# SSD mixer of a two-layer trunk: scores and decay as one product on a zero-padded tile, small copies on ScalarE, the transposed state in two tiles, no copy of the stacked rows

## The chip, the core and the metric

The kernel runs on one core of a Trainium2 chip. The metric is the device time of one execution in microseconds, the median of several runs. Engines are called TensorE (PE in the rows; PEld is its weight load), VectorE (DVE), ScalarE (ACT), GpSimd (POOL) and SyncE (SP, which issues most DMAs).

## What is computed

The reference is one inference step of a two-layer trunk on 512 prompt tokens and 8 x 8 sample tokens, 576 columns in all. Each layer has a SwiGLU block, a mixer, and another SwiGLU block. The mixer of layer 0 is the Mamba-2 SSD mixer that the change touches:

```python
def ssd_mixer(h, ssm0, conv0, w_in, conv_w, conv_b, dt_bias, a_log, d_skip, norm_g, w_out):
    proj = h @ w_in
    z, xbc, dt_raw = jnp.split(proj, [D_INNER, D_INNER + CONV_DIM], axis=-1)
    xbc, conv_new = causal_dwconv(xbc, conv0, conv_w, conv_b)      # width 4
    xbc = jax.nn.silu(xbc)
    xs, Bm, Cm = jnp.split(xbc, [D_INNER, D_INNER + SSD_GROUPS * D_STATE], axis=-1)
    ...
    y, ssm_new = ssd_scan(xs, dt, A, Bm, Cm, ssm0)
    y = y + d_skip.astype(f32)[:, None] * xs.astype(f32)
    y = y.reshape(bsz, l, D_INNER) * jax.nn.silu(z.astype(f32))
    yg = y.reshape(bsz, l, SSD_GROUPS, D_INNER // SSD_GROUPS)
    yg = yg * lax.rsqrt(jnp.mean(yg * yg, axis=-1, keepdims=True) + EPS)
    ...
# in ssd_scan, by chunks of 128 prompt tokens (8 for the samples):
    decay = jnp.exp(jnp.where(tril, seg, -jnp.inf))
    cb = jnp.einsum('bclgn,bcsgn->bclsg', Cc, Bc)
    y_diag = jnp.einsum('bclsgr,bcsgrp->bclgrp', cb[..., None] * decay, xdt)
    chunk_states = jnp.einsum('bcsgn,bcsgr,bcsgrp->bcgrpn', Bc, decay_end, xdt)
    h_final, h_starts = lax.scan(step, h_init, ...)
    y_off = jnp.einsum('bclgn,bclgr,bcgrpn->bclgrp', Cc, jnp.exp(a_cum), h_starts)
```

There are 8 groups of 4 heads; a head has 64 channels and a state of 64 x 128. New states, the last three rows before the convolution, and the token outputs are returned.

## The kernel before

Activations lie with channels on the 128 partitions and the 576 tokens along a row. The weights are read in float32 and split on the chip into a high and a low part (`block`: a cast on ScalarE, L317, and a subtraction, L318, which in this mixer GpSimd mostly does). A projection of one block of 128 channels (`proj`, `mm`, `passes`) is 48 matmuls of 288 columns into one of two PSUM accumulators (`acc`, two banks each); the split weights go through six buffers, two to a projection.

`ssd` loops over the groups g = 0 to 7. `conv_in(ct)` projects one block of the 32 convolved channel blocks. VectorE moves it out of the accumulator into `ext` (L637 to L639), in which the halo, the three rows before each sample sequence, is set in front (L636). The last three rows of each sequence go into `tails` (L641, L642). Then comes the convolution in `cacc`: one step on ScalarE (L645) and three on VectorE (L647). `ext` has two buffers.

`group(bt, ctl)` makes, once for each group, B transposed (`bnat`), the stacked B rows of the samples split into two parts (`bns`, `bsp`) and spread by a mask (`bblk`, GpSimd), and the scores `cbs` of B and C: 512 columns for the prompt and 64 x 64 for the samples.

`pair(g, j)` treats two heads at a time, 16 in all. It loads the state `nat`, transposes it on TensorE (L789) and copies it into `h0t`, one half by ScalarE and one by VectorE (L790); eight small matmuls of C with it (L795) follow. The decays `m` come by DMA, are masked on GpSimd (L808 to L810), put through the exponential on ScalarE (L813) and multiplied by the scores on VectorE (L814, L815); the products with `xdt` are L871 and L873. The running state of the chunks is `ht` (L853, L857), used by L864.

Groups 2, 4 and 6 also run eight blocks of the output projection (`outproj`, with `yn`), four ahead of each pair, each a unit of 24 matmuls (12 in group 2) that VectorE adds to `x` (L414), which frees the accumulator. The sum of squares of a group is `sqacc` (L949), which TensorE reduces over the partitions (L184). `spread` (L749) uses `rhs`, the end of a long chain on the step sizes in group 0.

No order is written out for most of this. A scheduler with a timeline of its own sets the order of each engine's instructions when the program is built, so any edit in the mixer can move others. Each engine then works through its own list in order.

Of the kernel before, what the change touches and what calls it, by code (L numbers as in the profile page):

```python
# [8 lines left out]
F32 = mybir.dt.float32  # L9
F32R = mybir.dt.float32r  # L10
I32 = mybir.dt.int32
AF = mybir.ActivationFunctionType
ALU = mybir.AluOpType
# [4 lines left out]
P = 128  # L18
D = 1024
KD = D // P  # L20
SEQ = 512
NB = 8
# [27 lines left out]
def trunk(ctx, tc, x_prompt, x_sample, state_ssm, state_conv, state_pool,  # L50
# [536 lines left out]
    def ssd(tail):  # L587
# [5 lines left out]
        with ExitStack() as st:  # L593
# [37 lines left out]
            def conv_in(ct):  # L631
# [4 lines left out]
                V.tensor_copy(out=es[:, :, 0:3], in_=cst[:, ct].rearrange("p (b e) -> p b e", e=3))  # L636
# [5 lines left out]
                V.tensor_copy(out=tails[:, ct, 3:27].rearrange("p (b e) -> p b e", e=3), in_=es[:, :, XST - 3:XST])  # L642
# [136 lines left out]
            def pair(g, j, bt, ctl, bnat, bblk, cbs, xst, yt):  # L779
# [5 lines left out]
                h0t = wk.tile([P, NB, P], F32, name="h0t", bufs=1)  # L785
                for q in range(2):
                    pt = misc()
                    for i in range(4):
                        PE.transpose(out=pt[:, i * P:(i + 1) * P], in_=nat[:, 4 * q + i], identity=ident)  # L789
                    (V.tensor_copy if q else S.copy)(out=h0t[:, 4 * q:4 * q + 4], in_=pt.rearrange("p (b n) -> p b n", n=P))  # L790
                pq = misc()
                for b in range(NB):
                    r = b % 4 * 32
                    o = SEQ + b // 4 * 32
                    PE.matmul(out=pq[r:r + 32, (2 + b // 4) * P:(3 + b // 4) * P], lhsT=ctl[:, o:o + 32], rhs=h0t[:, b], start=True, stop=True)  # L795
# [18 lines left out]
                V.tensor_tensor(out=m[:, :, 0:SEQ], in0=m[:, :, 0:SEQ], in1=cbs[:, 0:SEQ].unsqueeze(1).broadcast_to([P, 2, SEQ]), op=ALU.mult)  # L814
                V.tensor_tensor(out=ms, in0=ms, in1=cbs[0:64, SEQ:T].unsqueeze(1).broadcast_to([64, 2, 64]), op=ALU.mult)  # L815
# [101 lines left out]
            def group(bt, ctl):  # L917
                bnat = gp.tile([P, 4, P], F32, name="bnat")
                bns = gp.tile([96, 2, P], F32, name="bns")
                bsp = gp.tile([96, 2, P], F32, name="bsp")  # L920
                bblk = gp.tile([96, 2, 4, P], F32R, name="bblk")
                cbs = gp.tile([P, T], F32, name="cbs")
# [6 lines left out]
                S.copy(out=bns, in_=pt[0:96, 0:2 * P].rearrange("s (q n) -> s q n", q=2))  # L929
                S.copy(out=bsp.bitcast(F32R), in_=bns)  # L930
                V.tensor_tensor(out=bsp[32:64].bitcast(F32R), in0=bns[32:64], in1=bsp[32:64], op=ALU.subtract)
# [8 lines left out]
                S.copy(out=cbs[0:64, SEQ:T], in_=pt[0:64, 0:64])  # L940
                return bnat, bblk, cbs
# [30 lines left out]

            ys = None
# [246 lines left out]
```

## Time and profile before

| | us |
|---|---|
| median of 3 runs | 2354.91 (2354.45 to 2358.41) |
| profiled execution, its own time | 2357.4 |
| its span, first to last instruction | 2355.6 |
| TensorE busy | 2282.7 (97%) |
| VectorE busy | 1874.8 (80%) |
| ScalarE busy | 1053.1 (45%) |
| GpSimd busy | 1030.7 (44%) |

The mixer's work lies between about 428 and 1003 us. A row of the profile groups instructions by source line, engine and operands; after the bar it gives their busy time, the mean of one, and how long the engine stood idle just before them and for whom. A wait names the instruction that came last.

### The profile page before, as it was taken

What the parts mean: (1) busy time and instruction counts of PE and PEld (TensorE: products, weight loads), DVE (VectorE), ACT (ScalarE), POOL (GpSimd) and SP (SyncE); (2) the same over time, 40 slices, a digit from 0 to 9 for tenths busy, and PEclk for the clock granted to TensorE, in tenths of its full rate; (3) what the DMA queues carried; (4) which work ended last, traced back from release to release, by engine and by line L of the source; (5) the groups of instructions that cost most, each with busy time, mean ns of one, the idle gap of its engine ahead of it and who ended that gap; (6) DMA issues with size and microseconds to landing.
All of it is one profiled execution on the core that took longest, in us unless ns stands there. A gap on an engine that the chain in (4) does not pass through costs nothing.

```text
span 2355.6 us, 43789 instructions
## 1 busy us (share of the span) xinstructions
PE 2282.7 (97%) x17572; PEld 2241.3 (95%) x17572; DVE 1874.8 (80%) x2950; ACT 1053.1 (45%) x1947; POOL 1030.7 (44%) x796
## 2 busy tenths in 40 slices
PE   8999999999999999989999999999999999999998
PEld 7999999988999999979999999999999899999997
DVE  8987778688887786798877799778876859778876
ACT  6444434455554545354444354334444344344433
POOL 4555440344444444155554535555531325555530
PEclk9999999999999999999999999999999999999999
DMA  5223222243443334412232232323222242322221
GB/s 150 90 90 108 81 90 66 62 138 110 134 135 107 118 110 113 116 57 88 90 108 82 89 99 72 108 64 99 90 81 67 67 117 83 108 68 94 90 73 59
DMA packets 272904, 222.23 MB, mean 94 GB/s; under 512 B 8322, under 2 KB 269042, under 8 KB 272701
## 3 DMA queue, kind: packets, MB, share of 16 engines
q1 hardware_dynamic: 269172, 218.04, 30.4%
q8 instruction: 139, 2.28, 0.4%
q10 hardware_dynamic: 3528, 1.39, 0.2%
q14 instruction: 65, 0.52, 0.1%
HBM read 206.46 MB, written 12.94 MB: 93 GB/s over the span
## 4 chain that ended last, share of the span: by engine, by line
PE 60%; DVE 9%; ACT 1%; DMA 1%; issue 1%; DVEq 0%; SPq 0%; ACTq 0%
PE acc L375 29%; PE acc L339 27%; DVE wh L256 1%; PE acc L554 1%; DVE cacc L647 1%; PE acc L479 1%; DVE ws L1102 1%; DVE m L814 0%; DMA rd<-in_pool_w_out 0%; PE misc L871 0%; DVE wb L318 0%; PE misc L851 0%; PE misc L864 0%; DVE glo L256 0%; ACT m L813 0%
## 5 line engine op out<-in xcount | busy, mean ns | idle before, releaser
L375 PE MATMUL acc<-wh,wb 128*128 128x288 f32 x6888 | 920.4, 295 | 4.2 <-DVE fo L380 2.3
L375 PEld LDWEIGHTS acc<-wh,wb 128*128 128x128 f32 x6888 | 916.1, 189 | 5.9 <-ACT wb L317 3.2
L339 PE MATMUL acc<-ghi,wb 128*128 128x288 f32 x2752 | 550.7, 295 | 0.3 <-DVE x L416 0.3
L339 PEld LDWEIGHTS acc<-ghi,wb 128*128 128x128 f32 x2752 | 441.2, 188 | 0.6 <-DVE x L416 0.5
L317 ACT CAST wb<-raw 128x512 fp32r<-128x512 f32 (+1 forms) x440 | 265.7, 607 | 358.8 <-PE acc L339 151.9
L339 PE MATMUL acc<-glo,wb 128*128 128x288 f32 x1376 | 404.2, 295 | 0.0
L339 PE MATMUL acc<-hhi,wb 128*128 128x288 f32 x1824 | 382.8, 300 | 2.3 <-DVE x L414 0.8
L318 POOL TENSOR_TENSOR wb<-raw,wb 128x512 fp32r<-128x512 f32 (+1 forms) x154 | 211.3, 1374 | 339.5 <-ACT wb L317 330.5
L318 DVE TENSOR_TENSOR wb<-ws,wb 128x512 fp32r<-128x512 f32 x328 | 325.8, 1004 | 15.0 <-ACT wb L317 14.9
L318 DVE TENSOR_TENSOR wb<-raw,wb 128x512 fp32r<-128x512 f32 (+1 forms) x286 | 269.3, 956 | 63.8 <-ACT wb L317 63.3
L317 ACT CAST wb<-ws 128x512 fp32r<-128x512 f32 x328 | 202.5, 621 | 241.0 <-PE acc L375 216.8
L339 PEld LDWEIGHTS acc<-hhi,wb 128*128 128x128 f32 x1824 | 297.8, 190 | 5.7 <-issue 1.6
L416 DVE SCALAR_TENSOR_TENSOR x<-acc,x 128x576 f32<-128x576 f32 x160 | 120.6, 754 | 194.8 <-PE acc L339 194.6
L339 PE MATMUL acc<-hlo,wb 128*128 128x288 f32 x912 | 273.4, 300 | 0.0
L356 POOL TENSOR_TENSOR ws<-raw,ws 128x512 f32<-128x512 f32 x82 | 151.9, 1852 | 246.0 <-DVE wb L318 241.0
L339 PEld LDWEIGHTS acc<-glo,wb 128*128 128x128 f32 x1376 | 257.9, 188 | 0.0
L318 POOL TENSOR_TENSOR wb<-rd,wb 128x512 fp32r<-128x512 f32 x128 | 174.8, 1374 | 184.0 <-ACT wb L317 183.8
L317 ACT CAST wb<-rd 128x512 fp32r<-128x512 f32 x196 | 114.0, 592 | 250.1 <-PE acc L339 219.3
L355 POOL TENSOR_TENSOR ws<-raw 128x512 f32<-128x512 f32 x82 | 124.6, 1520 | 160.4 <-DVE wb L318 160.4
L339 PEld LDWEIGHTS acc<-hlo,wb 128*128 128x128 f32 x912 | 173.0, 190 | 0.8 <-issue 0.2
L353 POOL TENSOR_TENSOR ws<-raw 128x512 f32<-128x512 f32 x82 | 128.4, 1566 | 87.5 <-DMA raw<-in_ffn_w_gate 78.4
L354 POOL TENSOR_TENSOR ws<-ws,raw 128x512 f32<-128x512 f32 x82 | 130.3, 1589 | 7.7 <-DVE wb L318 1.5
(329 smaller groups left out, 2897.5 us busy)
## 6 DMA issues: line engine op xcount, KB each, us to landing
raw<-in_ffn_w_gate SPq DMA_DIRECT2D x41, 1024.0 KB
raw<-in_ffn_w_up SPq DMA_DIRECT2D x41, 1024.0 KB
rd<-in_ffn_w_down SPq DMA_DIRECT2D x80, 512.0 KB
raw<-in_ssd_w_in SPq DMA_DIRECT2D x48, 512.0 KB
m<-ad SPq DMA_DIRECT2D x16, 576.0 KB
nat<-in_state_ssm SPq DMA_DIRECT2D x16, 512.0 KB
out<-nat SPq DMA_DIRECT2D x16, 512.0 KB
raw<-in_ssd_w_out SPq DMA_DIRECT2D x24, 256.0 KB
```

Of the source, the lines that this page charges most:

```text
L256: V.scalar_tensor_tensor(out=o, in0=xs, scalar=g, in1=sub, op0=ALU.mult, op1=ALU.subtract)
L317: S.copy(out=hi, in_=src)
L318: (eng or V).tensor_tensor(out=lo, in0=src, in1=hi.bitcast(F32), op=ALU.subtract)
L339: PE.matmul(out=pd[:, h, 0:HALF], lhsT=lt, rhs=a[:, h * HALF:(h + 1) * HALF], start=first and n == 0, stop=last and n == 3 * len(acts) - 1)
L353: G.tensor_tensor(out=s[0], in0=blk[2], in1=blk[3], op=ALU.add)
L354: G.tensor_tensor(out=s[1], in0=s[0], in1=blk[0], op=ALU.subtract)
L355: G.tensor_tensor(out=s[2], in0=blk[2], in1=blk[0], op=ALU.subtract)
L356: G.tensor_tensor(out=s[3], in0=blk[1], in1=s[1], op=ALU.subtract)
L375: PE.matmul(out=pt[:, m, 0:HALF], lhsT=wb[:, j, k], rhs=hh[k, h][:, slot], start=n == 0, stop=n == 11)
L416: V.scalar_tensor_tensor(out=halves(x[:, d]), in0=pt[:, :, 0:HALF], scalar=scale, in1=halves(x[:, d]), op0=ALU.mult, op1=ALU.add)
L479: PE.matmul(out=pd[:, m, 0:HALF], lhsT=w[:, a, 2 * k + m], rhs=b[:, h * HALF:(h + 1) * HALF], start=n == 0, stop=n == 5)
L554: PE.matmul(out=pt[:, m, 0:HALF], lhsT=wb[:, a, k], rhs=hh[k, b][:, slot], start=q == 0 and k == a == b == 0, stop=q == 1 and k == 3 and a ...
```

## The change

Five edits, all in `ssd`:

- The halo copy into `ext` (L636) and the copy of the samples' last rows into `tails` (L642) go from VectorE to ScalarE, 32 of each.
- `h0t` becomes two tiles of four sequences each instead of one tile of eight.
- `cbs` is one tile for all groups, whose lower right corner (partitions 64 to 127 of the samples' columns) is set to zero once, so that the decays are multiplied by the scores in one operation of 128 x 2 x 576 instead of two. The samples' scores are copied into it by VectorE instead of ScalarE.
- `bns` is gone. ScalarE casts the stacked rows from PSUM, and VectorE's subtraction reads them from there as well.

```diff
                 G.memset(ext[:, 0:3], 0.0)
-                V.tensor_copy(out=es[:, :, 0:3], in_=cst[:, ct].rearrange("p (b e) -> p b e", e=3))
+                S.copy(out=es[:, :, 0:3], in_=cst[:, ct].rearrange("p (b e) -> p b e", e=3))
...
                 S.copy(out=tails[:, ct, 0:3], in_=ext[:, SEQ:SEQ + 3])
-                V.tensor_copy(out=tails[:, ct, 3:27].rearrange("p (b e) -> p b e", e=3), in_=es[:, :, XST - 3:XST])
+                S.copy(out=tails[:, ct, 3:27].rearrange("p (b e) -> p b e", e=3), in_=es[:, :, XST - 3:XST])
...
-                h0t = wk.tile([P, NB, P], F32, name="h0t", bufs=1)
+                h0t = [wk.tile([P, 4, P], F32, name=f"h0t{k}", bufs=1) for k in range(2)]
...
-                    (V.tensor_copy if q else S.copy)(out=h0t[:, 4 * q:4 * q + 4], in_=pt.rearrange("p (b n) -> p b n", n=P))
+                    (V.tensor_copy if q else S.copy)(out=h0t[q], in_=pt.rearrange("p (b n) -> p b n", n=P))
...
-                V.tensor_tensor(out=m[:, :, 0:SEQ], in0=m[:, :, 0:SEQ], in1=cbs[:, 0:SEQ].unsqueeze(1).broadcast_to([P, 2, SEQ]), op=ALU.mult)
-                V.tensor_tensor(out=ms, in0=ms, in1=cbs[0:64, SEQ:T].unsqueeze(1).broadcast_to([64, 2, 64]), op=ALU.mult)
+                V.tensor_tensor(out=m, in0=m, in1=cbs.unsqueeze(1).broadcast_to([P, 2, T]), op=ALU.mult)
...
-                S.copy(out=bns, in_=pt[0:96, 0:2 * P].rearrange("s (q n) -> s q n", q=2))
-                S.copy(out=bsp.bitcast(F32R), in_=bns)
-                V.tensor_tensor(out=bsp[32:64].bitcast(F32R), in0=bns[32:64], in1=bsp[32:64], op=ALU.subtract)
+                S.copy(out=bsp.bitcast(F32R), in_=pt[0:96, 0:2 * P].rearrange("s (q n) -> s q n", q=2))
+                V.tensor_tensor(out=bsp[32:64].bitcast(F32R), in0=pt[32:64, 0:2 * P].rearrange("s (q n) -> s q n", q=2), in1=bsp[32:64], op=ALU.subtract)
...
-                S.copy(out=cbs[0:64, SEQ:T], in_=pt[0:64, 0:64])
-                return bnat, bblk, cbs
+                V.tensor_copy(out=cbs[0:64, SEQ:T], in_=pt[0:64, 0:64])
+                return bnat, bblk
...
+            cbs = gp.tile([P, T], F32, name="cbs")
+            V.memset(cbs[64:P, SEQ:T], 0.0)
             ys = None
             for g in range(8):
```

The new source is two lines shorter, so from L815 on an instruction has a slightly smaller line number in the new program (L931 becomes L927, L949 becomes L945). The rebuilt order differs in many places in the mixer. Three of them follow.

VectorE at the start of group 1, before; `sqacc` is the sum of squares, `m` the decays, `rm` and `rr` the inverse root of the norm:

```order
L949 TENSOR_TENSOR sqacc<-sqacc,sq 128x576
L937 COPY cbs<-misc 128x512
L931 TENSOR_TENSOR bsp<-bns,bsp 32x256
L814 TENSOR_TENSOR m<-m,cbs 128x2x512 x2
L815 TENSOR_TENSOR m<-m,cbs 64x2x64 x2
L189 TENSOR_SCALAR rm<-misc 128x5
L190 TENSOR_SCALAR rr<-rm 128x5
L192 TENSOR_TENSOR rt<-rr 128x5
L790 COPY h0t<-misc 128x512
```

and now:

```order
L945 TENSOR_TENSOR sqacc<-sqacc,sq 128x576
L927 TENSOR_TENSOR bsp<-misc,bsp 32x256
L933 COPY cbs<-misc 128x512
L936 COPY cbs<-misc 64x64
L814 TENSOR_TENSOR m<-m,cbs 128x1152 x2
L189 TENSOR_SCALAR rm<-misc 128x5
L190 TENSOR_SCALAR rr<-rm 128x5
L790 COPY h0t_5916<-misc 128x512
```

Both pairs' multiplies stand together; the samples' scores now come from VectorE itself, just ahead of them, and the two L815 are gone.

VectorE at the start of group 4, before; `ext` is read out of the accumulator of a projection, `acc_8319` is that of the first block of the output projection:

```order
L937 COPY cbs<-misc 128x512
L647 SCALAR_TENSOR_TENSOR cacc<-ext,cw,cacc 128x600
L814 TENSOR_TENSOR m<-m,cbs 128x2x512 x2
L931 TENSOR_TENSOR bsp<-bns,bsp 32x256
L647 SCALAR_TENSOR_TENSOR cacc<-ext,cw,cacc 128x600
L637 TENSOR_TENSOR ext<-acc_8231,rb 128x288
L949 TENSOR_TENSOR sqacc<-sqacc,sq 128x576
L638 TENSOR_TENSOR ext<-acc_8231,rb 128x224
L639 TENSOR_TENSOR ext<-acc_8231,rb 128x8x8
L815 TENSOR_TENSOR m<-m,cbs 64x2x64 x2
L636 COPY ext<-cst 128x8x3
L414 TENSOR_TENSOR x<-acc_8319,x 128x576
```

and now, where the same block is `acc_8306`:

```order
L923 COPY bnat<-misc 128x512
L647 SCALAR_TENSOR_TENSOR cacc<-ext,cw,cacc 128x600
L927 TENSOR_TENSOR bsp<-misc,bsp 32x256
L933 COPY cbs<-misc 128x512
L945 TENSOR_TENSOR sqacc<-sqacc,sq 128x576
L637 TENSOR_TENSOR ext<-acc_8218,rb 128x288
L638 TENSOR_TENSOR ext<-acc_8218,rb 128x224
L639 TENSOR_TENSOR ext<-acc_8218,rb 128x8x8
L936 COPY cbs<-misc 64x64
L814 TENSOR_TENSOR m<-m,cbs 128x1152 x2
L414 TENSOR_TENSOR x<-acc_8306,x 128x576
```

The sum and the reads of the accumulator have moved ahead of the two multiplies.

ScalarE a little later in group 4, before; `xst` is the activated x block, `s` a stack of its sample columns:

```order
L913 ACT_TABLE_LOAD
L913 ACTIVATE xst<-cacc 128x512
L914 ACTIVATE xst<-cacc 128x64
L317 CAST wb<-raw 128x512
L775 COPY s_8504<-xst 128x192
L641 COPY tails<-ext 128x3
L645 ACTIVATE cacc<-ext,cols,cw 128x600
```

and now:

```order
L912 ACT_TABLE_LOAD
L912 ACTIVATE xst<-cacc 128x512
L913 ACTIVATE xst<-cacc 128x64
L636 COPY ext<-cst 128x8x3
L317 CAST wb<-raw 128x512
L641 COPY tails<-ext 128x3
L642 COPY tails<-ext 128x24
L645 ACTIVATE cacc<-ext,cols,cw 128x600
```

The halo copy stands behind an activation and ahead of a weight cast, the tail copy ahead of the first step of the convolution.

## Rows read from the trace of the kernel before

**Rows 1.** Stretch table: length, busy PE, PEld, DVE, ACT, POOL; clock; DMA.

```profile
428.00:1003.00 575.00, 551.35 (x4552) 524.40 (x4552) 456.58 (x1013) 287.39 (x615) 233.70 (x222) 0.98 0.40 116
```

**Rows 2.** Waits of TensorE from 428 to 1003: total us, times, longest.

```profile
PE misc L795 <- DVE h0t L790: 5.1, 3, 2.5
PE misc L749 <- DVE rhs L744: 4.9, 1, 4.9
PE acc L339 <- DVE ext L639: 3.8, 2, 2.3
PE misc L184 <- DVE sqacc L949: 3.0, 1, 3.0
PE acc L339 <- DVE x L414: 1.6, 4, 0.6
PE misc L864 <- DVE ht L857: 1.6, 2, 1.3
```

**Rows 3.** Stretch table of the half-clock stretches, columns as in group 1.

```profile
477.10:487.30 10.20, 9.13 (x45) 7.87 (x46) 7.14 (x16) 4.14 (x13) 6.37 (x8) 0.50 0.63 186
542.00:545.40 3.40, 3.40 (x17) 3.36 (x15) 3.23 (x11) 1.85 (x4) 0.36 (x1) 0.51 0.00 0
712.60:719.40 6.80, 6.26 (x43) 5.95 (x44) 6.76 (x18) 3.08 (x7) 2.77 (x4) 0.50 0.30 83
...
```

**Rows 4.** VectorE groups: shortest/median/longest ns; then groups with busy us, mean ns.

```profile
L642 DVE COPY tails<-ext x32: 158/178/1269, 432.5 to 948.2; 128x24 f32<-128x24 f32 x32
L815 DVE TENSOR_TENSOR m<-m,cbs x16: 274/300/1954, 490.5 to 939.1; 64x128 f32<-64x128 f32 x16
L931 DVE TENSOR_TENSOR bsp<-bns,bsp x8: 414/416/1406, 452.5 to 931.6; 32x256 fp32r<-32x256 f32 x8
L843 DVE SCALAR_TENSOR_TENSOR nat<-nat,decp,misc x128: 332/339/344, 506.2 to 972.9; 128x128 f32<-128x128 f32 x128
...
L642 DVE COPY tails<-ext 128x24 f32<-128x24 f32 x32 | 13.4, 418 | 0.3
L815 DVE TENSOR_TENSOR m<-m,cbs 64x128 f32<-64x128 f32 x16 | 10.8, 708 | 1.2 <-ACT cbs L940 1.2
L636 DVE COPY ext<-cst 128x24 f32<-128x24 f32 x32 | 9.2, 292 | 3.9 <-ACT cst L658 3.7
```

**Rows 5.** Timeline of group 1: start us, length, instruction, count, [idle before].

```profile
537.36 2.64 DVE L815 TENSOR_TENSOR m<-m,cbs 64x128 f32<-64x128 f32 x2 [1.18 <-ACT cbs L940]
...
538.24 0.43 PE L795 MATMUL misc<-h0t,ctl 128*32 128x128 f32 x8
```

**Rows 6.** Timeline of VectorE in group 4.

```profile
705.26 0.83 DVE L647 SCALAR_TENSOR_TENSOR cacc<-ext,cw,cacc 128x600 f32<-128x600 f32 x1
706.02 2.35 DVE L814 TENSOR_TENSOR m<-m,cbs 128x1024 f32<-128x1024 f32 x2
708.39 1.40 DVE L931 TENSOR_TENSOR bsp<-bns,bsp 32x256 fp32r<-32x256 f32 x1
709.83 1.74 DVE L647 SCALAR_TENSOR_TENSOR cacc<-ext,cw,cacc 128x600 f32<-128x600 f32 x1
...
711.86 1.22 DVE L949 TENSOR_TENSOR sqacc<-sqacc,sq 128x576 f32<-128x576 f32 x1
```

**Rows 7.** Timeline of TensorE in group 6: one unit of the output projection.

```profile
847.39 3.35 PE L339 MATMUL acc<-yn,wb 128*128 128x288 f32 x24
```

**Rows 8.** Timeline of VectorE in group 7.

```profile
934.52 4.44 DVE L814 TENSOR_TENSOR m<-m,cbs 128x1024 f32<-128x1024 f32 x2
```

**Rows 9.** Timeline of VectorE at the end of the step-size chain.

```profile
476.94 0.32 DVE L736 TENSOR_TENSOR nat<-nat 128x160 f32<-128x160 f32 x1 [3.21 <-ACT nat L735]
```

**Rows 10.** One ScalarE line: shortest/median/longest ns.

```profile
L641 ACT COPY tails<-ext x32: 177/193/196, 432.4 to 948.1; 128x3 f32<-128x3 f32 x32
```

**Rows 11.** Waits of GpSimd and ScalarE from 428 to 1003.

```profile
POOL ext L635 <- DVE cacc L647: 33.0, 20, 3.9
...
ACT wb L317 <- PE acc L339: 113.5, 63, 4.1
```

More of the change, by code (lines that the diff above doesn't have):

```diff
@@ L777, in stack, with pair @@
                     PE.transpose(out=pt[0:96, q * P:(q + 1) * P], in_=s3[:, q].rearrange("p a s -> p (a s)"), identity=ident)
-            def pair(g, j, bt, ctl, bnat, bblk, cbs, xst, yt):
+            def pair(g, j, bt, ctl, bnat, bblk, xst, yt):
                 h0 = 4 * g + 2 * j
@@ L794, in pair @@
                     o = SEQ + b // 4 * 32
-                    PE.matmul(out=pq[r:r + 32, (2 + b // 4) * P:(3 + b // 4) * P], lhsT=ctl[:, o:o + 32], rhs=h0t[:, b], start=True, stop=True)
+                    PE.matmul(out=pq[r:r + 32, (2 + b // 4) * P:(3 + b // 4) * P], lhsT=ctl[:, o:o + 32], rhs=h0t[b // 4][:, b % 4], start=True, stop=True)
                 ch = wk.tile([P, 2, P], F32, name="ch", bufs=1)
@@ L918, in group @@
                 bnat = gp.tile([P, 4, P], F32, name="bnat")
-                bns = gp.tile([96, 2, P], F32, name="bns")
                 bsp = gp.tile([96, 2, P], F32, name="bsp")
                 bblk = gp.tile([96, 2, 4, P], F32R, name="bblk")
-                cbs = gp.tile([P, T], F32, name="cbs")
                 pt = misc()
```

## The prediction

> **What bounds the kernel now.** I read the stretch table first, then who TensorE waits for, then the places one by one. The diff touches only the SSD mixer, and in the rebuilt program the first TensorE instruction that moves stands shortly after 428 us and the last before 1003 us; outside it TensorE's order is the same. In this stretch of 575 us TensorE is busy 551.35 us [rows 1], so 23.65 us are idle. The matmuls themselves are untouched, so the change can win only that idle time and what the clock loses after it. Nearly all of the idle time ends on VectorE [rows 2]: the transposed state `h0t`, the chain that makes `rhs`, the reads of a projection bank into `ext`, the sum `sqacc`, the running state `ht`. VectorE is busy 456.58 of the 575 us [rows 1], ScalarE half. So VectorE is late at a few places, not everywhere. After four of the waits the granted clock falls to the lower of its two levels, 1.2 of 2.4 GHz, with a granted share of 0.50 or 0.51; TensorE is busy 9.13, 6.26 and twice 3.40 us in these stretches [rows 3]. At half the clock about half of that is loss: 22.19 / 2 = 11.1 us. All that the change can reach is therefore 23.65 + 11.1 = 34.7 us, 1.5% of the run.
>
> **What VectorE loses and gets.** The 32 tail copies take 13.4 us and the 32 halo copies 9.2 us [rows 4]; the 16 small multiplies L815 take 10.8 us. A tail copy has a median of 178 ns but goes up to 1269; L815 has 300 and up to 1954; the subtraction L931, both of whose inputs lie in SBUF, has 416 and up to 1406, while 128 updates L843, which read one input from PSUM, stay within 332 to 344 ns [rows 4]. So the stretched ones are waiting for something, and reading PSUM avoids it: I take L931 at its median afterwards. Added are 128 columns in each of 16 multiplies (two of 1024 columns take 2.35 us, [rows 6], so 0.15 us more each, 2.4 us) and eight 64-column copies from PSUM, about 0.2 us each (estimate, between the 178 ns copy and the 0.3 us multiply), 1.6 us. The relief is at least 64 x 0.178 + 16 x 0.300 - 4.0 = 12.2 us if every stretch moves on to the next instruction, and at most 13.4 + 9.2 + 10.8 - 4.0 = 29.4 us if the stretches go too. Only what stands ahead of a waiting TensorE counts, so I cost it by place.
>
> Group 1 (h0t). Before, VectorE runs the two large multiplies, then stands 1.18 us until ScalarE has copied the 64-column scores, then needs 2.64 us for two L815 [rows 5], then copies `h0t`; TensorE waits 2.5 us [rows 2] and then runs 3.4 us at half clock. Now the small copy is VectorE's own, right behind the large one, and the L815 are gone: 1.18 + 2.64 - 0.3 (wider multiplies) - 0.2 (copy) = 3.3 us earlier, more than the wait. Taken: 2.5 + 1.7 = 4.2 us. If the stretch of L815 lands on the merged multiplies instead, 2 us.
>
> Group 4 (sqacc) has the largest clean case. Ahead of the sum stand 2.35 us of multiplies, the stretched subtraction 1.40, a convolution step at 1.74 where a free one takes 0.83, and the sum itself 1.22 [rows 6]. In the new order the sum stands directly behind the score copy, ahead of both multiplies; the subtraction and the convolution step come earlier, some 1.3 us unstretched. The sum is ready (2.35 + 1.40 + 1.74) - 1.3 = 4.2 us earlier than TensorE got it, and it waited 3.0 [rows 2]. Late next would be L414, which now stands behind both merged multiplies and frees a bank; TensorE has a whole unit of 24 matmuls (3.35 us, [rows 7]) in hand, against 2.7 us of multiplies. Taken: 3.0 + 6.26 / 2 = 6.1 us; at least 1 us by the subtraction alone.
>
> The two waits for `ext` are 3.8 us together [rows 2]; the larger, 2.3 us, follows the unit of [rows 7] in group 6, where the order is that of group 4, and the three `ext` reads now also stand ahead of the multiplies. Taken 3.0, bounds 1 to 3.8. For `ht`, 1.3 of the 1.6 us [rows 2], I take 1.0: copies and L815 just ahead are gone. In group 7 the two multiplies take 4.44 us [rows 8], 2.1 more than two unstretched ones, and TensorE waits 2.5 us for the `h0t` behind them; the multiplies still read two SBUF tiles and stay ahead of `h0t`, so I take 1.2 us, bounds 0 and 2.5 + 1.7 = 4.2.
>
> The largest wait, 4.9 us for `rhs` [rows 2], stays: VectorE there stands 3.21 us for an exponential on ScalarE [rows 9], whose chain the change leaves. About 0.5 us of copies ahead goes. The small waits, 23.65 - (4.9 + 2.5 + 3.8 + 1.3 + 3.0 + 2.5) = 5.65 us, lose perhaps 1.2. The split of `h0t` lets the first four products start on ScalarE's half; the trace of group 1 shows them already running ahead of VectorE's half [rows 5], so I give it nothing, with the 2.5 us as bound.
>
> ScalarE gets 64 copies of about 0.19 us, the duration of its 3-column tail copy [rows 10]: 12.4 us, minus the copies `bns` and the small score copy. It is free for 288 us of the stretch [rows 1], 113.5 of them waiting for TensorE to return weight buffers [rows 11]; that covers the copies at zero. Without this cover each pair delays a convolution by 0.4 us. SyncE issues the same transfers, a few in another place among their neighbours; the same lead of the casts covers that.
>
> Sum: 0.5 + 4.2 + 3.0 + 1.0 + 6.1 + 1.2 + 1.2 = 17.2 us. A new order brings new waits. Nothing in the trace shows them; the nearest rows are the small waits (L414: 1.6 us in four, [rows 2]) and, far above, one like `sqacc` with its half clock, 6.1 us. I take two of 2 us, 4 us; bounds 0 and 12. Net 13.2 us. The profiled execution took 2357.4 us (span 2355.6 and 1.8 around it), so 2344.2; the median 2354.9 lies 2.5 lower, and so does my number: **2342 us**.
>
> **The rivals.**
> *The stretches only move on.* Behind every removed copy stands a convolution step or a multiply that can be stretched just as well; then the relief is the 12.2 us and it is spread over 575 us, where most of it shows nowhere. Against it: the waits at groups 1 and 4 end by order, not by stretches. Price: the lower bounds, in the order of the sum 0 + 2 + 1 + 0.3 + 1 + 0 + 0.5 = 4.8 us, and the new waits of 4 us eat them: 2354 us, no change. The Trainium skill ("SBUF — State Buffer", Who interferes with whom) says that a VectorE instruction with two SBUF inputs, or a copy in a two-port mode, and a GpSimd instruction that reads SBUF exclude each other, the later one waiting in full. The trace agrees (L931 at 416 or 1406 ns, L843 never over 344, [rows 4]), and by that rule a removed copy leaves its wait to the next such instruction: it would come out as this rival does.
> *All waits close.* With VectorE 5% emptier everything but `rhs` could fall away: 34.7 - 4.9 - 4.6 = 25 us, 2330. Against it: group 7 and the new order.
> *Slower: ScalarE's halo copy waits for VectorE.* It overwrites `ext`, and may only start when VectorE's last convolution step on the buffer is done. GpSimd's memset of the same buffer waits for just that, 33.0 us in 20 waits, up to 3.9 us [rows 11]. ScalarE would stand there instead, with weight casts, the exponentials of `m` and the half of `h0t` queued behind it. If all of that reached TensorE: 17.2 - 33.0, so 2371 us; it turns slower than before by over 0.2% once 22 of the 33 us get through. For it: the new order puts the copy ahead of casts. Against: it stands mostly right behind an activation that has already waited for the same convolution chain, and casts run several blocks ahead.
> **How the numbers follow.** The forecast (2335 to 2350) gets 0.50, all waits close (2328 to 2335) 0.14, stretches move on (2350 to 2359) 0.22, slower 0.14. The range runs from 2330 to 2358: it leaves out half of the second and the last, about 0.2. A measurement here can tell about 0.2%, 4.7 us, from no change: faster 0.64, same 0.22, slower 0.14.
>
> **What would show it.** Right: in the new trace TensorE's idle time in the stretch is about 10 us instead of 23.65; no wait for `sqacc`, at most one for `h0t` and one for `ext`; a single half-clock stretch at `rhs` and perhaps one more; the merged multiply at 1.35 us where unstretched; the subtraction never over 0.5 us; tail copies on ScalarE at 0.19 us. Wrong: idle time of 20 us or more under other names (the first rival), or ScalarE waiting tens of us for the convolution steps at L636, with TensorE waiting for ScalarE (the slower one). Durations of stages outside 428 to 1003 us should repeat within 1 or 2 us; if they differ more, the sum fails for another reason.

## The result and the profile after

The changed kernel takes 2338.89 us (median of 4 runs, 2336.99 to 2342.42) against 2356.34 us for the kernel before on the same chip: a ratio of 0.9918, 95% interval 0.9906 to 0.9930. It is 17.5 us faster, inside the predicted range and 3 us below the forecast of 2342. The forecast gain was 13.2 us, so the measured one is 4.3 us larger. The profiled execution of the changed kernel took 2342.42 us, its span is 2340.7.

The first row is from the stretch table of the changed kernel, with the columns of [rows 1]; then come TensorE's waits from 428 to 1003 us, as in [rows 2], and the one stretch of the mixer at half clock, as in [rows 3].

```profile
428.00:990.00 562.00, 548.17 (x4597) 524.02 (x4596) 435.28 (x946) 295.63 (x676) 225.30 (x225) 0.99 0.41 119
```

```profile
PE misc L749 <- DVE rhs L744: 5.9, 1, 5.9
...
PE misc L795 <- DVE h0t L790: 1.3, 2, 0.9
```

```profile
476.80:487.00 10.20, 8.44 (x43) 7.25 (x44) 5.83 (x14) 4.91 (x15) 6.29 (x9) 0.50 0.50 149
```

The mixer now ends earlier: the matmuls that ended at 1003 us before end at about 985 us, and from there to 990 us TensorE doesn't stand idle, so the first row holds all of the mixer's idle time. TensorE's idle time falls from 23.65 to 562.00 - 548.17 = 13.83 us, a gain of 9.8. Its busy time at half clock falls from 22.19 to 8.44 us, which is worth (22.19 - 8.44) / 2 = 6.9 us. Together that is 16.7 us. The waits for `sqacc` and `ext` are gone, those for `h0t` (1.3 us) and `ht` (0.3 us) nearly so; `rhs` got longer.

A second measure, which needs no estimate of the clock, is the distance between two marks on TensorE in the same two executions: the first L657 (the convolution's old rows, ahead of the mixer's moved work; the row of the line's instructions has the first and last start after its durations) and the L236 behind the wait for `rr` in the next block (a row of the timeline). The two of before, then the two of after:

```profile
L657 PE MATMUL misc<-ident,crow x32: 213/214/238, 427.4 to 441.5; 24*128 24x24 f32 x32
```

```profile
1051.29 0.69 PE L236 MATMUL misc<-ident,rr 128*128 128x128 f32 x2 [4.40 <-DVE rr L197]
```

```profile
L657 PE MATMUL misc<-ident,crow x32: 213/214/238, 428.0 to 442.1; 24*128 24x24 f32 x32
```

```profile
1033.20 0.69 PE L236 MATMUL misc<-ident,rr 128*128 128x128 f32 x2 [4.35 <-DVE rr L197]
```

That is 623.9 and 605.2 us: the mixer became 18.7 us shorter. I call this distance the mixer's length below. All of it is gained between the first L657 and the first L479 (the last matmuls on `yn`), a stretch that holds the same matmuls in both kernels. The rows of this stretch, before and after:

```profile
427.38:994.90 567.52, 544.56 (x4506) 517.87 (x4505) 452.40 (x1000) 287.20 (x615) 232.28 (x221) 0.98 0.41 117
```

```profile
428.03:976.87 548.84, 535.70 (x4506) 511.94 (x4505) 425.97 (x928) 289.81 (x663) 220.42 (x221) 0.99 0.42 121
```

Idle time fell by 9.8 us, as above, and TensorE's busy time by 8.9. So the 2 us beyond the 16.7 are busy time, more than half of the time at half clock accounts for; which matmuls got shorter was not followed.

The place in group 4 shows the new order at work (VectorE, then TensorE; compare [rows 6]):

```profile
700.95 1.08 DVE L945 TENSOR_TENSOR sqacc<-sqacc,sq 128x576 f32<-128x576 f32 x1
701.95 0.44 DVE L637 TENSOR_TENSOR ext<-acc,rb 128x288 f32<-128x288 f32 x1
...
702.61 0.21 DVE L639 TENSOR_TENSOR ext<-acc,rb 128x64 f32<-128x64 f32 x1
...
702.98 2.63 DVE L814 TENSOR_TENSOR m<-m,cbs 128x1152 f32<-128x1152 f32 x2
```

```profile
703.94 0.34 PE L184 MATMUL misc<-ones,sqacc 128*64 128x1 f32 x6
```

The sum and the three reads that free the accumulator stand ahead of both multiplies, the sum is ready at 702.03, and TensorE reaches it at 703.94 without waiting.

### The profile page after: what moved, and what is told of

It is laid out like the page before. It is cut to its first block, busy times and chain, and to the rows that moved or that the text cites. A ratio compares the mean times of both kernels' runs of the same rounds, so it can differ in the third digit from the quotient of the medians.

```text
span 2340.7 us, 43780 instructions
## 1 busy us (share of the span) xinstructions
PE 2279.8 (97%) x17572; PEld 2241.2 (96%) x17572; DVE 1841.8 (79%) x2879; ACT 1055.6 (45%) x1995; POOL 1019.4 (44%) x796
## 4 chain that ended last, share of the span: by engine, by line
PE 63%; DVE 9%; ACT 2%; DMA 1%; issue 1%; POOL 0%; DVEq 0%; SPq 0%; ACTq 0%; POOLq 0%
PE acc L339 29%; PE acc L375 28%; DVE cacc L647 1%; DVE wh L256 1%; PE acc L554 1%; PE acc L479 1%; DVE wb L318 1%; DMA m<-ad 1%; DVE ws L1100 1%; PE misc L870 1%; ACT m L813 1%; PE misc L850 0%; DMA rd<-in_pool_w_out 0%; PE misc L863 0%; PE misc L823 0%
## 5 line engine op out<-in xcount | busy, mean ns | idle before, releaser
L318 POOL TENSOR_TENSOR wb<-raw,wb 128x512 fp32r<-128x512 f32 (+1 forms) x154 | 204.9, 1332 | 320.6 <-ACT wb L317 315.0
```

Source lines behind the costliest of these rows:

```text
L318: (eng or V).tensor_tensor(out=lo, in0=src, in1=hi.bitcast(F32), op=ALU.subtract)
```

## Experiments

All kernels here compute the whole reference. Every one is compared with the kernel before on the same chip. The mixer's length is from one profiled execution each, by the two marks above; VectorE's busy time is that of the whole span, with the scatter of the later stages in it; where the text needs the mixer's alone, it takes the stretch from the first L657 to the first L479. Between executions with the same order of TensorE the mixer's length differs by up to 1.4 us (split alone against before; the changed kernel, its repetition below and "all but the split" lie at -18.7, -18.9 and -20.0), so differences of 1 or 2 us between kernels say little.

| kernel | median us | ratio to before (95%) | mixer's length, change in us | VectorE busy us |
|---|---|---|---|---|
| before | 2356.34 to 2359.70 beside these | 1 | 0 | 1874.8 |
| changed | 2338.89 | 0.9918 (0.9906 to 0.9930) | -18.7 | 1841.8 |
| copies alone | 2353.39 | 0.9975 (0.9964 to 0.9986) | -3.8 | 1856.1 |
| scores alone | 2361.24 | 1.0006 (0.9996 to 1.0017) | +2.7 | 1871.4 |
| rows alone | 2352.87 | 0.9974 (0.9964 to 0.9985) | -7.3 | 1885.2 |
| split alone | 2359.66 | 1.0003 (0.9994 to 1.0013) | +1.4 | 1876.0 |
| all but the copies | 2352.29 | 0.9971 (0.9961 to 0.9980) | -7.9 | 1877.5 |
| all but the scores | 2346.81 | 0.9951 (0.9937 to 0.9966) | -14.6 | 1849.8 |
| all but the rows | 2345.02 | 0.9946 (0.9931 to 0.9960) | -12.8 | 1860.4 |
| all but the halo copies | 2343.72 | 0.9940 (0.9923 to 0.9956) | -16.3 | 1858.8 |
| all but the split | 2338.75 | 0.9920 (0.9904 to 0.9936) | -20.0 | 1848.3 |

**Copies alone.** Edit against the kernel before:

```diff
-                V.tensor_copy(out=es[:, :, 0:3], in_=cst[:, ct]...
+                S.copy(out=es[:, :, 0:3], in_=cst[:, ct]...
...
-                V.tensor_copy(out=tails[:, ct, 3:27]...
+                S.copy(out=tails[:, ct, 3:27]...
```

> Only the halo and tail copies go to ScalarE; the rest is as before. Theory A (VectorE is late at a few places, and what stands ahead of them there decides): VectorE loses 64 copies (22.6 us of busy time), the convolution steps come earlier, so the wait for sqacc in group 4 and the two waits for ext shrink; the wait for the small score copy in group 1 stays. 8 us faster, 2344 to 2352. Theory B (the stretches only move to the next instruction): under 3 us, 2353 to 2357, with as many long L647 steps as there were long copies. Theory C (ScalarE's halo copy stands in its queue for VectorE and TensorE feels it): slower than 2359, with TensorE waits that end on ScalarE.

Measured: 0.25% faster, 5.6 us, between the first two theories. TensorE's longest wait in the mixer but `rhs`:

```profile
PE misc L795 <- DVE h0t L790: 6.7, 3, 4.0
```

The `ext` waits are gone, that for `sqacc` fell to 0.3 us, and VectorE is 17.7 us emptier in the mixer, but the mixer is only 3.8 us shorter: the wait for `h0t` at group 1 grew from 2.5 to 4.0 us, and those for `rhs` and L414 by 1.0 and 2.2 in all. Relief alone does not close a wait that stands behind the two multiplies.

**Scores alone.** Edit against the kernel before: one score tile, one multiply, the small copy on VectorE.

```diff
-                V.tensor_tensor(out=m[:, :, 0:SEQ], ...
-                V.tensor_tensor(out=ms, in0=ms, ...
+                V.tensor_tensor(out=m, in0=m, in1=cbs.unsqueeze(1).broadcast_to([P, 2, T]), op=ALU.mult)
...
-                S.copy(out=cbs[0:64, SEQ:T], in_=pt[0:64, 0:64])
+                V.tensor_copy(out=cbs[0:64, SEQ:T], in_=pt[0:64, 0:64])
```

> Only the scores: one zero-padded tile for all groups, one multiply instead of two, the small score copy on VectorE. Theory A: closes the h0t wait of group 1 with its half clock (4.2 us) and a part of those for sqacc and ext, as the small multiplies no longer stand ahead; 6 us faster, 2347 to 2354. Theory B: 0 to 2 us. If this edit carries most of the gain of the whole change (19 us), 2337 to 2343.

Measured: no difference that can be told from none. Two waits of TensorE, then VectorE and TensorE in group 4:

```profile
PE misc L184 <- DVE sqacc L947: 12.2, 2, 6.2
...
PE misc L795 <- DVE h0t L790: 0.6, 1, 0.6
```

```profile
707.51 4.76 DVE L814 TENSOR_TENSOR m<-m,cbs 128x1152 f32<-128x1152 f32 x2
712.19 0.44 DVE L637 TENSOR_TENSOR ext<-acc,rb 128x288 f32<-128x288 f32 x1
712.55 0.74 DVE L947 TENSOR_TENSOR sqacc<-sqacc,sq 128x576 f32<-128x576 f32 x1
...
713.35 1.24 PE L184 MATMUL misc<-ones,sqacc 128*64 128x1 f32 x20 [6.08 <-DVE sqacc L947]
```

The edit does what the sum said at group 1 (the `h0t` wait falls from 2.5 to 0.6 us, with its half clock), and gives it all back: in the order built for this edit the sum stands behind both merged multiplies, which are stretched to 4.76 us, and the same happens in group 6. TensorE waits 6 us each time and then runs 6.8 us at half clock.

**Rows alone.** Edit against the kernel before:

```diff
-                S.copy(out=bns, in_=pt[0:96, 0:2 * P]...
-                S.copy(out=bsp.bitcast(F32R), in_=bns)
-                V.tensor_tensor(out=bsp[32:64].bitcast(F32R), in0=bns[32:64], ...
+                S.copy(out=bsp.bitcast(F32R), in_=pt[0:96, 0:2 * P]...
+                V.tensor_tensor(out=bsp[32:64].bitcast(F32R), in0=pt[32:64, 0:2 * P]...
```

> Only the copy of the stacked rows is gone, so that the subtraction reads one input from PSUM. Theory A: it is never stretched any more (0.42 us each, up to 1.41 before), which takes 1 us from the chains of groups 4, 6 and 7: 2 to 4 us faster, 2351 to 2355. Theory B: the 1 us goes to the convolution step behind it, no difference, 2354 to 2358.

Measured: 0.26% faster, 6.1 us, above the first theory. The stretch from the first L657 to the first L479, with the columns of [rows 1]:

```profile
426.92:987.27 560.35, 538.35 (x4505) 511.51 (x4504) 457.86 (x1000) 283.55 (x607) 231.47 (x221) 0.99 0.41 119
```

VectorE is 5.5 us busier in the mixer than before (457.86 against 452.40) with as many instructions, so through stretched ones, and the mixer is still 7.3 us shorter. Nearly all of that is clock: idle time fell by 1.0 us only, but of the four half-clock stretches of [rows 3] the one at `rhs` alone is left. The `sqacc` wait is gone, though the sum still stands behind both multiplies. VectorE and TensorE in group 4 here, and then TensorE in the kernel before:

```profile
711.01 0.74 DVE L947 TENSOR_TENSOR sqacc<-sqacc,sq 128x576 f32<-128x576 f32 x1
...
706.17 5.68 PE L339 MATMUL acc<-yn,wb 128*128 128x288 f32 x41
711.81 0.75 PE L184 MATMUL misc<-ones,sqacc 128*64 128x1 f32 x20
```

```profile
713.14 1.23 PE L184 MATMUL misc<-ones,sqacc 128*64 128x1 f32 x20 [2.96 <-DVE sqacc L949]
```

In this order the reads of the accumulator stand ahead of the multiplies (L637 at 706.26, L814 at 707.07), and TensorE has two units of the output projection, 48 matmuls, ahead of L184 instead of one of 24. It arrives later and finds the sum ready. "Copies alone", "all but the scores" and "all but the rows" close this wait in the same way, with 48 matmuls ahead of L184; the changed kernel does it by the early sum, with 24. So how full VectorE is does not decide it, and neither does the place of the sum alone: it is the place of the sum against what TensorE still has to do.

**Split alone.** Edit against the kernel before:

```diff
-                h0t = wk.tile([P, NB, P], F32, name="h0t", bufs=1)
+                h0t = [wk.tile([P, 4, P], F32, name=f"h0t{k}", bufs=1) for k in range(2)]
```

> Only the transposed state in two tiles; no work is removed, but the order of the program is dealt anew. Theory A: 0 to 2 us, since the first four products already ran ahead of VectorE's half. It also shows what a new order alone does: if the time moves by more than 4 us either way, order as such is worth as much as the relief, and the sums by place say little.

Measured: nothing. The waits for `h0t` (5.1 us, longest 2.5), `rhs` (4.9), `ext` (3.8) and `sqacc` (3.0) are those of [rows 2] to the tenth in their sums; that for `ht` grew from 1.6 to 3.3 us. TensorE's sequence of matmuls is that of the kernel before, by lines and operands, so this run says nothing on what a new order does by itself.

The four edits alone sum to -3.8 + 2.7 - 7.3 + 1.4 = -7.0 us of mixer, against -18.7 for all. So some 12 us come from edits acting together, far more than the scatter. The next kernels leave one edit out of the changed kernel each.

**All but the copies.** Edit against the changed kernel:

```diff
-                S.copy(out=es[:, :, 0:3], in_=cst[:, ct]...
+                V.tensor_copy(out=es[:, :, 0:3], in_=cst[:, ct]...
...
-                S.copy(out=tails[:, ct, 3:27]...
+                V.tensor_copy(out=tails[:, ct, 3:27]...
```

> The whole change, but halo copies L636 and tail copies L642 stay on VectorE. Alone, the copies won 0.25%, the rows 0.26%, the scores and the split nothing; the whole won 0.8%, so about 0.3% comes from edits acting together. Theory A (the scores edit closes the wait at group 1 but in its own order puts the sum sqacc behind the multiplies; the rows edit brings the sum ahead again, so these two act together): ratio to before about 0.9945, 2345 us, no wait for sqacc, none over 1 us for h0t, the ext waits and some stretched convolution steps back. Theory B (the scores need VectorE empty, so the copies must go): the gain falls to that of the rows, ratio 0.9975, 2352 us, with a wait for h0t or sqacc of 2 us or more back.

Measured: 0.9971, the second theory's number, with another wait than it named. VectorE and TensorE in group 4:

```profile
706.51 3.69 DVE L814 TENSOR_TENSOR m<-m,cbs 128x1152 f32<-128x1152 f32 x2
...
710.78 0.21 DVE L639 TENSOR_TENSOR ext<-acc,rb 128x64 f32<-128x64 f32 x1
```

```profile
711.14 5.09 PE L339 MATMUL acc<-yn,wb 128*128 128x288 f32 x25 [2.38 <-DVE rm L189]
```

The sum is early, as in the first theory, but the three reads of the accumulator now stand behind the merged multiplies, and TensorE waits 2.4 us here and 3.8 us in group 6 (the row names L189, which ran beside the last read), each time with a half-clock stretch. So the copies are worth 10.8 us of mixer on top of the other edits and 3.8 alone. VectorE is nearly as busy as before (450.2 us in the mixer against 452.4) and the mixer 7.9 us shorter.

**All but the scores.** Edit against the changed kernel: the two multiplies, one score tile per group, and the small copy on ScalarE are back (the diff of "scores alone", reversed).

```diff
-                V.tensor_tensor(out=m, in0=m, ...
+                V.tensor_tensor(out=m[:, :, 0:SEQ], ...
+                V.tensor_tensor(out=ms, in0=ms, ...
```

> The whole change without the scores edit: separate multiplies L814 and L815, one score tile per group, the small score copy on ScalarE. Copies and rows alone won 5.6 and 6.1 us. Theory A (the scores edit is what closes group 1): wait for h0t at group 1 of 2.5 us or more with a half-clock stretch, ratio 0.9950, 2347 us. Theory B (VectorE's load decides, whatever relieves it): the h0t wait shrinks below 1 us, ratio 0.993, within 0.1% of the whole change.

Measured: 0.9951, close to the first theory. VectorE in group 1:

```profile
537.72 2.66 DVE L815 TENSOR_TENSOR m<-m,cbs 64x128 f32<-64x128 f32 x2
```

The two L815 take 2.66 us here as in [rows 5], and TensorE waits 2.0 us for the `h0t` behind them; the half-clock stretch that was expected did not follow. The scores edit is worth 4.1 us of mixer once the reads stand ahead of the multiplies, though alone it lost 2.7.

**All but the rows.** Edit against the changed kernel: `bns` is back.

```diff
-                S.copy(out=bsp.bitcast(F32R), in_=pt[0:96, 0:2 * P]...
+                S.copy(out=bns, in_=pt[0:96, 0:2 * P]...
+                S.copy(out=bsp.bitcast(F32R), in_=bns)
```

> The whole change, but the stacked rows are copied into bns first and the subtraction reads SBUF. Theory A: the subtraction is stretched again (up to 1.4 us, median 0.42) and ScalarE has 8 more copies; the sum sqacc comes late in some group, a wait of 2 us or more with half clock, ratio 0.9965, 2350 us. Theory B (the removed copy only matters through the order it happens to give, and the copies give another good one): no wait for sqacc, ratio 0.993.

Measured: 0.9946, between the two. There is no wait for `sqacc` (0.3 us), against the first theory; instead two waits of some 2 us stand at other places:

```profile
PE misc L789 <- issue: 2.3, 1, 2.3
PE misc L861 <- DVE ch L797: 2.1, 1, 2.1
```

```profile
534.71 1.23 DVE L192 TENSOR_TENSOR rt<-rr 128x5 f32<-128x5 f32 x1
535.98 1.96 DVE L193 TENSOR_TENSOR rt<-rt,rm 128x5 f32<-128x5 f32 x1
537.97 1.21 DVE L197 SCALAR_TENSOR_TENSOR rr<-rt,rr 128x5 f32<-128x5 f32 x1
```

Ahead of `ch` in group 1, three instructions on five columns take 4.4 us; unstretched they take 0.16 us each (the next L192, at 539.89, took 0.15). Each of the two waits brings a half-clock stretch. This is what the first rival foresaw: a stretch finds another instruction.

**All but the halo copies.** Edit against the changed kernel:

```diff
-                S.copy(out=es[:, :, 0:3], in_=cst[:, ct]...
+                V.tensor_copy(out=es[:, :, 0:3], in_=cst[:, ct]...
```

> The whole change, but the halo copy L636 stays on VectorE; only the tail copies go to ScalarE. In the changed kernel ScalarE stands 18.1 us in 8 waits of up to 3.4 us at L636 for VectorE's last convolution step on the buffer. Theory A (that wait is hidden by the lead of the weight casts): removing it wins nothing, VectorE gets 32 copies of about 0.28 us back, ratio 0.992 to 0.994, 2339 to 2344 us. Theory C (the wait costs): time falls below that of the changed kernel, ratio 0.990, 2335 us, and the waits for cacc on ScalarE's steps (22.0 us on VectorE in the changed kernel) fall to about half.

Measured: 0.9940, at the slow end of the first theory. ScalarE's wait at L636, 18.1 us in the changed kernel, is gone, and the time does not fall: the waits for `cacc` on VectorE go from 22.0 to 17.5 us, not to half. ScalarE's wait is hidden, and moving the halo copies is no loss; the 2.4 us of mixer that they seem worth are near the scatter, and the intervals of the two ratios overlap.

**All but the split.** Edit against the changed kernel:

```diff
-                h0t = [wk.tile([P, 4, P], F32, name=f"h0t{k}", bufs=1) for k in range(2)]
+                h0t = wk.tile([P, NB, P], F32, name="h0t", bufs=1)
```

> The whole change, but the transposed state stays one tile of eight sequences. Alone the split won nothing. Theory A (the split only lets products start that already ran ahead): ratio to before 0.991 to 0.993, within 0.1% of the whole change, 2336 to 2341 us, and the waits for h0t are as in the changed kernel, 1.3 and 0.9 us. Rival (in the emptier program the split lets TensorE start on ScalarE's half while VectorE is still late): the waits for h0t grow by 2 us or more and a half-clock stretch comes back at one of them, ratio 0.994 or more, 2344 us.

Measured: 0.9920, the same as the changed kernel; the waits for `h0t` are 1.4 and 0.9 us. The split is worth nothing, in company too.

**The changed kernel again, and two tries at `rhs`.** These three ran beside each other on one chip. The second only moves a line: `spill(ad)`, six DMA issues of ScalarE, goes behind the two exponentials.

```diff
-            spill(ad, ac)
...
             S.activation(out=e, in_=ac, func=AF.Exp)
+            spill(ad, ac)
             spill(ed, e)
```

The third does this too and holds TensorE's spread products back, by small matmuls on the convolution of block 17, which is issued earlier:

```diff
-                        spread()
+                        pre[17] = conv_in(17)
+                        spread(pre[17])
...
-            def spread():
+            def spread(late):
                 pt = misc()
+                PE.matmul(out=pt[0:32, 0:32], lhsT=late[:, 0:32], rhs=late[:, 0:32], start=True, stop=True)
```

> The changed kernel again, unaltered, beside the two that follow. Its profiled execution was the slowest of its four runs and had longer half-clock stretches behind the mixer than the kernel before had there. Theory A (that is scatter of the clock in stages the change does not touch): here the mixer's end marker (the idle time before L236) stands again about 18 us earlier than before, and the half-clock stretches after the mixer have their old lengths in at least some runs; median 2336 to 2341 us. Rival (the change lengthens later stages): the same long stretches return at the same places.

> The changed kernel with one move: the two exponentials L735 and L737 are issued on ScalarE ahead of the six DMAs of spill(ad), which took 2.7 us of ScalarE's queue in front of them. Nothing is left out. The rebuilt order also moves the spread product (L749) 23 matmuls, about 3 us, earlier on TensorE. Theory A (the DMA issues set the rhs wait of 5.9 us): the chain ends 2.7 us earlier and the wait falls to about 3 us, time 2336. Theory B (TensorE's own place for L749 moves with it): the wait stays at 5 to 6 us because TensorE arrives 3 us earlier too, time within 0.1% of the changed kernel.

> As the run with the exponentials first, but the projection of block 17 is issued ahead of the spread, and three 32-column matmuls on its convolution hold the spread products back on TensorE, so that they stand about where the changed kernel has them. Nothing is left out. If the six DMA issues are what the rhs wait of 5.9 us consists of, and the place on TensorE is kept, the wait falls to 2 to 3.5 us, with a half-clock stretch of the same length or none: 2.5 to 7 us less than the changed kernel, ratio to it 0.997 to 0.999. If VectorE's own chain sets it (scan, exponentials, ext reads, the stretched L744), the wait stays above 4.5 us and the time is that of the changed kernel; two further table loads on ScalarE (1.3 us each) could even make it slower.

| kernel | median us (range) | ratio to before (95%) | mixer's length, change in us |
|---|---|---|---|
| changed, again | 2337.93 (2337.65 to 2341.63) | 0.9907 (0.9891 to 0.9922) | -18.9 |
| exponentials first | 2345.08 (2342.43 to 2346.06) | 0.9935 (0.9922 to 0.9947) | -16.6 |
| and spread held back | 2336.21 (2334.39 to 2338.28) | 0.9900 (0.9886 to 0.9914) | -24.4 |

The changed kernel repeats, in the time and in the mixer's length. The chain at `rhs` in the changed kernel (VectorE, then ScalarE), and, with the exponentials first, its end and two of TensorE's waits:

```profile
475.16 0.33 DVE L736 TENSOR_TENSOR nat<-nat 128x160 f32<-128x160 f32 x1 [3.99 <-ACT nat L735]
475.41 0.45 DVE L637 TENSOR_TENSOR ext<-acc,rb 128x288 f32<-128x288 f32 x1
...
476.07 2.43 DVE L744 TENSOR_TENSOR rhs<-nat,mh 32x64 f32<-32x64 f32 x2
```

```profile
470.78 1.74 ACTq L727 DMA_DIRECT2D ad<-nat  x4
472.55 0.92 ACTq L729 DMA_DIRECT2D ad<-nat  x2
473.50 1.28 ACT L735 ACT_TABLE_LOAD   x1 [4.53 <-DMA ad<-nat]
```

```profile
471.18 0.53 DVE L744 TENSOR_TENSOR rhs<-nat,mh 32x64 f32<-32x64 f32 x2
```

```profile
PE misc L749 <- DVE rhs L744: 3.7, 1, 3.7
...
PE misc L863 <- DVE ht L856: 2.6, 1, 2.6
```

With the exponentials first the chain ends at 471.7 instead of 478.5, 6.8 us earlier: the six issues (2.66 us) and the table load (1.28, now ahead of the data) are out of it, and `rhs` stands ahead of the `ext` reads, unstretched. TensorE reaches its products 4.5 us earlier too (468.1 instead of 472.6), so the wait only falls from 5.9 to 3.7 us, and a new wait of 2.6 us for `ht`, with a half-clock stretch, comes in group 0. The kernel is 7 us slower than the changed one, which neither theory had. Why its median lost more than the 2.3 us of its mixer was not followed. With the products held back the wait is 3.0 us, within the 2 to 3.5 expected, but it is now the small matmuls' wait for the convolution; `rhs` is ready at 474.05, 2.2 us before it ends. There is no wait for `rhs` any more, and the mixer is 5.5 us shorter than in the changed kernel beside it; the medians differ by 1.7 us only, less than the 2.5 to 7 expected, and the intervals overlap, so this version is the fastest run here but isn't shown to beat the changed kernel.

## Why the prediction was right, step by step

The sum by places, in us gained (idle time plus half of the time at half clock):

| step | forecast | measured |
|---|---|---|
| `rhs` | 0.5 | -1.0 + 0.35 = -0.65 |
| group 1, `h0t` | 4.2 | 2.5 - 0.33 + 1.7 = 3.9 |
| `ext` | 3.0 | 3.8 |
| `ht` | 1.0 | 1.3 - 0.3 = 1.0 |
| group 4, `sqacc` | 6.1 | 3.0 + 3.1 = 6.1 |
| group 7, `h0t` | 1.2 | 2.5 - 0.94 + 1.7 = 3.3 |
| small and new waits | 1.2 - 4.0 = -2.8 | 5.65 - 6.3 = -0.7 |
| sum | 13.2 | 16.7 |

The terms missed by -1.2 to +2.1 us each, and the misses partly offset each other; that the sum came within 3.5 us of these rows, and the time within 3 us of the forecast, is in part luck.

*What bounds it* held: the gain lies in idle time and clock of the mixer, and the matmuls did not change. The forecast of "about 10 us" of idle time was too low (13.8), that of one half-clock stretch at `rhs` was right.

*Group 1 and group 4* came out by order as worked out: the small copy waits for nobody, L815 is gone, and the sum stands ahead of the multiplies. "Scores alone" and "all but the scores" show the first, the group 4 rows the second. Group 4 had another way out, which the prediction did not look at: the two units of the output projection ahead of L184, as in "rows alone".

*The `rhs` step failed in its sign.* The prediction left the chain as it was and took 0.5 us of copies off. VectorE does get the exponential earlier, L736 at 475.16 instead of 476.94 [rows 9], but ends the chain 0.8 us later. Before, the three `ext` reads ran while VectorE waited for the exponential, and L744 came right behind L736:

```profile
472.86 0.45 DVE L637 TENSOR_TENSOR ext<-acc,rb 128x288 f32<-128x288 f32 x1
...
477.19 0.53 DVE L744 TENSOR_TENSOR rhs<-nat,mh 32x64 f32<-32x64 f32 x2
```

In the new order two of the reads stand behind L736, inside the chain (0.66 us), and L744 takes 2.43 us for its two halves instead of 0.53, beside subtractions of GpSimd that start at 475.94. This comes with the halo copies: in all six executions with them on ScalarE and the exponentials at their old place the reads stand behind L736 and L744 takes 2.43 us; in all six with them on VectorE the reads stand ahead of it and L744 takes 0.52 or 0.53. In "all but the halo copies" the wait is 4.9 us again. Work that cost nothing inside a wait can come to stand behind the wait in a new order.

*Group 7* was sized too low: I kept the multiplies' stretch, and it went. They take 2.61 us instead of the 4.44 of [rows 8], but the instruction behind them is stretched in their place:

```profile
921.78 2.61 DVE L814 TENSOR_TENSOR m<-m,cbs 128x1152 f32<-128x1152 f32 x2
924.32 1.25 DVE L190 TENSOR_SCALAR rr<-rm 128x5 int32<-128x5 int32 x1
925.49 0.68 DVE L790 COPY h0t<-misc 128x512 f32<-128x512 f32 x1
```

*New waits* were taken at 4 us, against 1.2 us that the small ones would lose; the small and new ones together grew by 0.7 us only. That and group 7, 2.1 us each, are most of what the sum was short of.

*Costs and durations.* The groups that answer to [rows 4] and [rows 10], shortest, median and longest in ns:

```profile
L814 DVE TENSOR_TENSOR m<-m,cbs x16: 1340/1380/2644, 489.3 to 923.1; 128x1152 f32<-128x1152 f32 x16
L927 DVE TENSOR_TENSOR bsp<-misc,bsp x8: 417/417/420, 452.0 to 916.9; 32x256 fp32r<-32x256 f32 x8
L642 ACT COPY tails<-ext x32: 198/216/220, 433.2 to 934.0; 128x24 f32<-128x24 f32 x32
```

The merged multiply has the 1.35 us forecast where unstretched, the subtraction that reads PSUM is never stretched, and the tail copies on ScalarE take 0.22, not 0.19. The Trainium skill ("SBUF — State Buffer", Who interferes with whom) says that a VectorE instruction with at most one SBUF input, outside the two-port modes, doesn't contend with GpSimd; L927 agrees, 769 ns on average before and 417 now. VectorE's busy time in the mixer fell by 26.4 us (452.40 to 425.97), inside the 12.2 to 29.4 forecast; of the 33.0 us over the whole span the rest is scatter of the other stages (26.9 in the repetition).

*The first rival* (stretches move on) happened in part. The eight L190 on five columns took 2.4 us before and take 6.6 now. They grew by 4.2 us and L744 by 1.9, against 7.7 (L642), 6.0 (L815) and 2.9 (L931) of stretch that left, by their busy time less the count times the median. Most of the stretch left for good, since the 26.4 us are nearer to the upper bound. It did not decide the time, though at `rhs` a stretch did land on an instruction that TensorE waits for.

*The slower rival* had its wait, and no effect:

```profile
ACT ext L636 <- DVE cacc L647: 18.1, 8, 3.4
```

ScalarE stands there for the convolution steps as described, but the weight casts run ahead; with the halo copies back on VectorE nothing is won.

*What the prediction did not see* is that the terms are not separate. It gave 4.2 us to the scores edit, 3.0 to the copies. Alone, the scores edit lost 2.7 us of mixer and the copies won 3.8; together with the rows they make up the whole gain. The sum by places was made on the order of the finished program; a sum by edits would have come out wrong. Left untested: no run relieves VectorE with the order kept, or changes TensorE's order alone, so what each of the two is worth by itself stays open.

*Outside the mixer* the stages were to repeat within 1 or 2 us. From the mark at L236 to the end it is 2355.6 - 1051.29 = 1304.3 us before and 1307.5 after; over all 14 profiled executions this part lies between 1303.5 and 1307.9. One cause is the clock, which falls at other places: 375 us behind the mark TensorE runs 3.4 us at half clock before. In the profiled execution of the changed kernel the same place runs at full clock, and 14 us later, behind a wait of 2.73 us for L197, come 6.9 us at half clock; its repetition has the 3.4 us at the old place again. Before, then the two places after:

```profile
1426.00:1429.40 3.40, 3.40 (x15) 3.40 (x16) 3.40 (x11) 1.49 (x3) 0.00 (x0) 0.50 0.00 0
```

```profile
1408.10:1411.50 3.40, 3.40 (x29) 3.40 (x27) 3.40 (x11) 1.86 (x4) 0.00 (x0) 1.00 0.00 0
1422.20:1429.10 6.90, 6.90 (x30) 6.50 (x31) 4.56 (x7) 1.92 (x4) 1.58 (x1) 0.51 0.01 2
```

So the bound of 1 or 2 us was somewhat too tight: these stages scatter by 4 us without any edit in them.

## What to carry to other kernels

Where a scheduler rebuilds the order, cost a change by the places at which the bounding engine waits, on the finished program's order, and don't add up the edits: here four edits that sum to 7 us alone gave 18.7 together. Relieving a busy engine counts only for what stands ahead of a waiting one: "rows alone", with VectorE 5.5 us busier in the mixer, and "copies alone", with it 17.7 us emptier, came out equally fast (0.9974 and 0.9975). Small reads that free an accumulator belong ahead of long elementwise work: in "rows alone" TensorE then runs on to a second unit. And a step at which the bounding engine already waits should be looked at again for work that the new order moves from inside the wait to behind it.

## What the runs showed of the hardware

The loss of clock behind a wait does not follow from the length of the wait alone. In "all but the rows" a wait of 2.07 us for `ch`, at 539.17 us, was followed by 3.4 us at half clock; in "rows alone" one of 2.91 us for `ext`, at 846.01 us, by none. TensorE's stretch behind the first, and the 10 us around the second:

```profile
542.60:546.00 3.40, 3.40 (x18) 3.40 (x17) 3.29 (x9) 0.45 (x2) 0.56 (x2) 0.50 0.00 0
```

```profile
846.00:856.00 10.00, 7.09 (x62) 6.76 (x61) 9.97 (x24) 4.49 (x11) 2.78 (x4) 1.00 0.20 54
```

The outer stages show it without any change of the program there. Ahead of the place at 1426 us TensorE waits 1.03, 0.60 and 0.16 us before, and 1.02, 0.61 and 0.16 us in the changed kernel ahead of 1408; the first was followed by half clock and the second was not. So up to half of a wait's price hangs on something other than the wait, and the terms with a clock part (group 1, 4 and 7) were less certain than the sum made them look. A stretch also has little to do with an instruction's size: L190, on five columns, takes 0.17 us alone and 1.25 us in group 7 above, while GpSimd works on a subtraction of weights (1.90 us from 923.65).
